# Output projection by seven products for each pair of channel tiles, h sums on VectorE, and early loads into pools that stay open

## The chip, the core and the metric

The kernel runs on one core of one Trainium2 chip, as one program. Its time is device microseconds. All figures in float32: weights and activations are float32 in HBM, and each number that TensorE multiplies is held as a pair of float32r tiles, a rounded high part and the rest.

TensorE (PE) multiplies, VectorE (DVE), ScalarE (ACT) and GpSimd (POOL) compute elementwise, SyncE (SP) issues the transfers in the order of its own queue. A static order of instructions stands for each engine; semaphores make an engine wait for another.

## The reference, cut to what matters

```python
z = h @ lp['w_in']                      # h: adaLN-modulated RMSNorm of x, (1024 tokens, 1024)
q = na_query(z, lp['q_norm_g'])         # 8 heads of 64
k, v = na_kv(z[..., A_K:A_Z], lp['k_norm_g'])
ya = neighbourhood_attention(q, k, v, kc, vc, lp['rpb']) * silu(z[..., A_Z:B_B])
yb = short_conv_branch(z, lp['conv_short_w'])
yc = conformer_branch(z, ...)           # 31-tap conv, layer norm, silu, gate
ga, gb, gc = jnp.split(jax.nn.sigmoid(z[..., GATES:]), N_BRANCH, axis=-1)
m = ga * (ya @ w_out_a) + gb * (yb @ w_out_b) + gc * (yc @ w_out_c)
x = x + gate * (m @ w_o)                # the output projection, 1024 x 1024 by 1024 x 1024
```

## The kernel before, in words

All activations lie transposed: 128 channels on the partitions, 1024 tokens along the free axis. h is kept in eight tiles ha (tokens 0 to 511) and eight tiles hb (512 to 1023), each with a high and a low half; hlf[o][k] is the tile of token half o and channel tile k. A product of two such pairs is three matmuls of 128x512 (high by high, high by low, low by high), in `mm3` or `product`.

The stages, by the span of the profiled execution: adaLN and the first projections to 123 us; four attentions, one for two heads each, with the projections for the next heads and the conv inputs as other work for TensorE, to 542; the Strassen stage to 943; the three merges to 1107; the output projection to 1195. A scheduler lays out each engine's order ahead of time from the program text, with its own timeline; `issue_after(x)` holds a group back until x is in the order. Tile pools decide which wait an instruction then needs: a tile with n buffers is given again only when the readers of the tile n before are done.

*Attention.* `attend(hp)` goes over 2 heads, 4 column blocks and 2 halves, so 16 half-steps for a pair of heads; they are counted 1 to 64 over the four attentions, and the last attention has 49 to 64. A half-step is sc and sl (scores of context and local window) on TensorE, mn and the local part of pbuf on VectorE (`TENSOR_REDUCE mn<-sc` opens it), two exponentials on ScalarE, pp (transposes by `ident`), ph and plo (the pair), py (the product with v), ya (its sum). GpSimd makes the bias image for it.

*Plain tiles.* `plain(ct, dst)` is a projection of h that ends in SiLU or Sigmoid: eight products into zaps for each token half (24 matmuls), `flt` from `tmp`, and a transfer out. ZA and BZ tiles stand in the text behind the last attention and two gate tiles stand later; the scheduler puts their matmuls between those of the last attention. zaps has two banks (ps_m); `tmp` is the pool rp with 6 buffers, shared by flt and hsum.

*h_sums(j)* makes the sums and differences of h blocks that the Strassen stage needs: four wholes (high + low), four differences, each stored to td. It is called once after each attention.

*Strassen stage.* A projection for two channel tiles and two token halves is a 2x2 block product; `group` and `last_two` do it by seven products (ga, gc, gd, ge and so on) instead of eight. T1 to T3 and T4 are the split td blocks: `load_t` brings each into a staging tile traw and splits it; T4 goes into the hb tiles 0 to 3. Weights come by wr, are split into wh and wl, and their block sums s stand on GpSimd. Beside it VectorE does the 31-tap conv (L690) and the results of the attention are gated (`a_result`, zb and a_result halves).

*Merges and projection.* `merge(1)`, `merge(0)`, `merge(2)` in this order: for each of eight channel tiles dm and token halves b, four products (ops) of wout with yb, ya or yc; mt sums them under the gates gs. The layer norm of the third branch (`norm_steps`, steps given out by `beside_b` and `beside_a`) runs beside the first two; its sums over channels are matmuls with ones (sums), its rstd is spread by matmuls with a diagonal (diag). yb and ya come back from DRAM through `loaded_y`, cv through cvin. Then for each of eight channel tiles and two token halves fin adds eight products of wo and the split mt (mh, ml), and L1116 does gate and residual.

Of the kernel before, what the change touches and what calls it, by code (L numbers as in the profile page):

```python
# [17 lines left out]
P = 128  # L18
D = 1024
KT = 8  # L20
# [22 lines left out]
def tile_hybrid(ctx: ExitStack, tc, x, xT, cx, cond, crow, ng, w_ada, b_ada, wqkv, wz,  # L43
# [5 lines left out]
    hctx = ExitStack()  # L49
    hp_pool = hctx.enter_context(tc.tile_pool(name="hT", bufs=1))  # L50
# [79 lines left out]
    def qkv(hp, w=None, cts=None, first=(), psc=None, mid=None):  # L130
# [41 lines left out]
        def context():  # L172
            vc = [a1.tile([P, 2, P], F32R, tag=f"vc{h}", name="vc") for h in range(2)]
# [64 lines left out]
    A_t = cst.tile([P, KT, 2], F32, name="A_t")  # L238
    B_t = cst.tile([P, KT, 2], F32, name="B_t")
# [224 lines left out]
    with tc.tile_pool(name="at", bufs=1, reuse_waits="tile") as at, \  # L464
# [45 lines left out]
        def attend(hp):  # L510
            ya = at.tile([P, 16, 64], F32, tag="ya", name="ya", bufs=1)
            for h in range(2):
# [9 lines left out]
                for cb in range(4):  # L522
# [54 lines left out]
                    dve.tensor_tensor(out=ya[hs, :, cb * 16 : cb * 16 + 16],  # L577
# [16 lines left out]
        def h_sums(j):  # L594

            def whole(o, k):
                t = tmp("hsum")
                pool.tensor_tensor(out=t, in0=hlf[o][k][:, 0].bitcast(F32), in1=hlf[o][k][:, 1].bitcast(F32), op=ALU.add)
                return t

            def less(i, a, b):

                pool.tensor_tensor(out=b, in0=a, in1=b, op=ALU.subtract)
                nc.sync.dma_start(td[i][j], b)
# [22 lines left out]

    sctx = ExitStack()
# [34 lines left out]
    for i in (1, 0, 2):  # L663
        load_t(T[i], i)
    load_t(T4, 3)
# [99 lines left out]

    def last_two(cts, uses):
# [24 lines left out]
        for n in two:  # L791
# [4 lines left out]
            dve.tensor_tensor(out=x[n], in0=f, in1=x[n], op=ALU.add)  # L796
        s3 = [s_(n, raw[n][0], raw[n][2], ALU.subtract, "s3") for n in two]
# [7 lines left out]
        for n in two:  # L805
# [5 lines left out]
            uses[n][1](0, y[n])  # L811
        s4 = [s_(n, raw[n][1], s2[n], ALU.subtract, "s4") for n in two]
# [90 lines left out]

    for i in range(4):
        u = b_start(i)
        gate_pair()
        b_end(i, u)
    halves = [(i, b) for i in range(4) for b in range(2)]
    for i in range(5):
# [5 lines left out]
        for _ in range(1 + (i in (0, 2, 4))):  # L915
            a_result(*halves.pop(0))
# [7 lines left out]
    hctx.close()  # L924


    wp = ctx.enter_context(tc.tile_pool(name="w2", bufs=9, side="right", reuse_waits="tile"))
    state["wp"] = wp
    kinds = (("mt", 8), ("cv", 4), ("ya0", 4), ("yb", 8), ("ya1", 4), ("bp", 0))
    pools = {n: (ctx.enter_context(tc.tile_pool(name=n, bufs=1, reuse_waits="tile")), k) for n, k in kinds}  # L930
    bp = pools["bp"][0]
# [3 lines left out]
    def big(name, n=S, dt=F32):  # L935
        return bp.tile([P, n], dt, tag="big", name=name, bufs=10)

    def of(kind, name, dt=F32R):
        p, k = pools[kind]
        return p.tile([P, S], dt, tag=kind, name=name, bufs=k)  # L940
# [13 lines left out]
    def loaded_y(n, i, name):  # L954
        out = []
        for h in range(2):
            t = of(("ya0", "ya1")[i // 2] if n else "yb", name)
            nc.sync.dma_start(t.bitcast(F32), ysd[n][i][h])
            out.append(t)
        return out  # L960

# [4 lines left out]
    def merge(br, ys, beside=lambda dm, b: None):  # L966
        for dm in range(KT):
            w = load_w(wout[br, dm], 4, dve if dm % 2 else pool)
# [233 lines left out]
```

## Time and profile before

| | us |
|---|---|
| median of 3 runs (lowest, highest) | 1202.31 (1201.91, 1203.02) |
| profiled execution, its span | 1200.33, 1198.5 |
| TensorE busy (share of the span) | 1126.9 (94%) |
| VectorE | 850.8 (71%) |
| ScalarE | 560.8 (47%) |
| GpSimd | 663.4 (55%) |
| HBM read, written | 120.62 MB, 46.14 MB |
| mean granted TensorE clock | 0.964 |

The prediction shows rows of several views. A stretch row gives start and end, its length, busy time and count of instructions for PE, PE weight loads, DVE, ACT and POOL, then the granted clock of TensorE, the mean busy share of the DMA engines and GB/s. A wait row gives the engine and line that waited, the one that ended the wait, and total us, times, longest. A row of a group gives the line, engine, operation and tiles, the count, and least, median and greatest duration in ns or, behind a bar, busy us and the mean. A row of the timeline begins with start and duration in us.

### The profile page before, as it was taken

How to read it: one execution, taken by the hardware profiler on the slowest of the kernel's cores; microseconds unless marked ns; L12 is line 12 of the kernel's file. 1: busy time of each engine (PE TensorE's matmuls, PEld its weight loads, DVE VectorE, ACT ScalarE, POOL GpSimd, SP SyncE). 2: the span in 40 equal slices, each digit the busy share in tenths (PEclk: the TensorE clock that was granted, in tenths of full speed). 3: DMA queues.
4: the chain of work that ended last, by engine and by line, in shares of the span. 5: the costliest groups of instructions: out<-in, count | busy, mean ns of one | idle time of the engine just before them, and what ended most of it. 6: DMA issues, size and time to landing. Idle time of an engine off the chain costs nothing.

```text
span 1198.5 us, 16663 instructions
## 1 busy us (share of the span) xinstructions
PE 1126.9 (94%) x5566; PEld 961.0 (80%) x5566; DVE 850.8 (71%) x1495; ACT 560.8 (47%) x1167; POOL 663.4 (55%) x623
## 2 busy tenths in 40 slices
PE   5779699999999999998999999999999798999998
PEld 4678699899899788886788888887877476888887
DVE  7995768788877875657993897896993356679311
ACT  5575358557656688784333332324334335313110
POOL 6675845645745833310887677868888006851110
PEclk7789899999999999999899999999999798999999
DMA  9235242332322313117234434345653694662621
GB/s 354 106 136 180 72 126 84 104 108 85 111 64 77 118 63 121 56 42 236 93 102 142 124 105 149 101 154 173 190 192 132 242 406 153 205 241 88 237 80 53
DMA packets 88151, 167.87 MB, mean 140 GB/s; under 512 B 11008, under 2 KB 39424, under 8 KB 88064
## 3 DMA queue, kind: packets, MB, share of 16 engines
q1 hardware_dynamic: 83456, 164.70, 40.9%
q10 hardware_dynamic: 4608, 2.10, 0.6%
q8 instruction: 44, 0.72, 0.3%
q14 instruction: 43, 0.35, 0.1%
HBM read 120.62 MB, written 46.14 MB: 139 GB/s over the span
## 4 chain that ended last, share of the span: by engine, by line
PE 59%; DVE 17%; DMA 8%; POOL 7%; issue 4%; ACT 3%; SPq 1%; POOLq 0%; DVEq 0%; ACTq 0%
DVE cv L690 4%; PE ops L107 4%; PE ops L109 4%; PE ops L108 4%; PE pp L564 3%; PE zaps L108 3%; PE zaps L107 3%; PE zaps L109 3%; PE ps L109 3%; PE ps L107 3%; PE ps L108 3%; PE fin L109 2%; PE fin L107 2%; PE fin L108 2%; DMA wada<-in_w_ada 2%
## 5 line engine op out<-in xcount | busy, mean ns | idle before, releaser
L90 POOL TENSOR_TENSOR wl<-wr,wh 128x384 fp32r<-128x384 f32 (+2 forms) x93 | 89.6, 969 | 182.2 <-ACT wh L88 156.1
L690 DVE SCALAR_TENSOR_TENSOR cv<-upad,cf_t,cv 128x512 f32<-128x512 f32 x240 | 166.9, 747 | 0.2
L88 ACT CAST wh<-wr 128x384 fp32r<-128x384 f32 (+2 forms) x138 | 61.2, 456 | 113.5 <-DMA wr<-in_wout 46.9
L533 POOL TENSOR_TENSOR bias<-mka,vimg 128x288 f32<-128x288 bf16 (+1 forms) x64 | 59.5, 931 | 87.8 <-DVE mn L547 76.5
L639 POOL TENSOR_TENSOR wl<-s,wh 128x512 fp32r<-128x512 f32 x57 | 79.5, 1409 | 11.1 <-ACT wh L638 6.4
L638 ACT CAST wh<-s 128x512 fp32r<-128x512 f32 x76 | 46.1, 616 | 75.6 <-POOL s L642 64.1
L639 POOL TENSOR_TENSOR wl<-wr,wh 128x512 fp32r<-128x512 f32 x46 | 64.4, 1402 | 22.7 <-ACT wh L638 22.7
L569 DVE TENSOR_TENSOR plo<-pp,ph 128x512 fp32r<-128x512 f32 (+1 forms) x96 | 60.8, 640 | 8.5 <-ACT ph L567 8.0
L714 PE MATMUL ga<-ha,wh 128*128 128x512 f32 x152 | 60.6, 398 | 6.5 <-ACT wh L638 4.7
L564 PE MATMUL pp<-ident,pbuf 128*128 128x128 f32 x352 | 59.1, 273 | 1.6 <-DVE pbuf L553 1.3
L716 PE MATMUL ga<-ha,wl 128*128 128x512 f32 x152 | 60.3, 397 | 0.2 <-POOL wl L639 0.2
L715 PE MATMUL ga<-ha,wh 128*128 128x512 f32 x152 | 60.2, 396 | 0.0
L567 ACT CAST ph<-pp 128x512 fp32r<-128x512 f32 (+1 forms) x96 | 51.7, 547 | 16.8 <-PE pp L564 16.0
L549 ACT ACTIVATE pbuf<-sc,mn 128x256 f32<-128x256 f32 x64 | 30.4, 475 | 60.1 <-DVE mn L547 59.6
L1116 DVE SCALAR_TENSOR_TENSOR o<-fin,gate,xr 128x512 f32<-128x512 f32 x16 | 12.0, 751 | 59.7 <-PE fin L109 59.7
L551 DVE TENSOR_TENSOR mn<-mn 128x1 f32<-128x1 f32 x64 | 17.6, 275 | 47.0 <-ACT pbuf L550 46.7
L109 PE MATMUL fin<-mh,wl 128*128 128x512 f32 x128 | 49.8, 389 | 0.0
L108 PE MATMUL fin<-ml,wh 128*128 128x512 f32 x128 | 49.8, 389 | 0.0
L107 PE MATMUL fin<-mh,wh 128*128 128x512 f32 x128 | 49.7, 389 | 0.0
L564 PEld LDWEIGHTS pp<-ident,pbuf 128*128 128x128 f32 x352 | 42.7, 140 | 7.0 <-DVE pbuf L553 2.6
L90 DVE TENSOR_TENSOR wl<-wr,wh 128x384 fp32r<-128x384 f32 (+2 forms) x45 | 31.6, 705 | 13.9 <-ACT wh L88 13.9
L79 POOL TENSOR_TENSOR ssh<-ssh,half_neg 128x4 f32<-128x4 f32 (+1 forms) x40 | 39.4, 987 | 2.7
(382 smaller groups left out, 3970.3 us busy)
## 6 DMA issues: line engine op xcount, KB each, us to landing
wr<-in_wz SPq DMA_DIRECT2D x36, 512.0 KB, 3.9
gs<-gd SPq DMA_DIRECT2D x24, 512.0 KB, 5.2
wada<-in_w_ada SPq DMA_DIRECT2D x16, 512.0 KB, 8.7
wr<-in_wz SPq DMA_DIRECT2D x36, 192.0 KB, 2.5
cht<-chd SPq DMA_DIRECT2D x24, 256.0 KB, 3.1
gd<-gate SPq DMA_DIRECT2D x22, 256.0 KB, 3.1
vimg<-in_rpbs SPq DMA_DIRECT2D x16, 288.0 KB, 3.0
gd<-c SPq DMA_DIRECT2D x18, 256.0 KB, 3.1
```

The lines of the kernel that those rows point to most:

```text
L88: act.copy(hi[:, :n], raw[:, :n])
L90: state["lo"] = lo_eng.tensor_tensor(out=lo[:, :n], in0=raw[:, :n], in1=hi[:, :n].bitcast(F32), op=ALU.subtract)
L107: pe.matmul(ps, ah, bh, start=i == 0, stop=False)
L108: pe.matmul(ps, ah, bl, start=False, stop=False)
L109: pe.matmul(ps, al, bh, start=False, stop=i == n - 1)
L564: pe.transpose(out=pp[:, c * 256 + hf * P : c * 256 + hf * P + P], in_=pts[hf][:, o : o + P], identity=ident)
L569: dve.tensor_tensor(out=plo[:, : m * 256], in0=pp[:, : m * 256], in1=ph[:, : m * 256].bitcast(F32), op=ALU.subtract)
L639: eng.tensor_tensor(out=lo, in0=src, in1=hi.bitcast(F32), op=ALU.subtract)
L690: dve.scalar_tensor_tensor(out=acc[b], in0=src, scalar=cf_t[:, i, j : j + 1], in1=acc[b], op0=ALU.mult, op1=ALU.add)
L714: pe.matmul(ps, wh, bh, start=first and j == 0, stop=False, skip_group_check=True)
L715: pe.matmul(ps, wh, bl, start=False, stop=False, skip_group_check=True)
L716: pe.matmul(ps, wl, bh, start=False, stop=last and j == 3, skip_group_check=True)
```

## The change

Four things change together.

- h_sums for all four j is called after the loop over heads, held back until the last ya of the third attention is in the order; its additions are VectorE's, not GpSimd's.
- The T blocks have a pool of their own (tp), opened before the Strassen stage and never closed, and load in place: the block comes into the low half and is split there. T1 to T3 load before the last two plain tiles, T4 at the first loop of the second half. The tiles of h (hT) stay open to the end.
- a_result is spread: one in each of three more loops instead of two in some. In last_two, yb is loaded after the f products and cvin before the last ones, into T and hb tiles; the first ya loads go with the merges' other tiles (`of`, `homes`). The layer-norm steps are cut and paced otherwise; the diagonal matmuls are one for each half.
- The output projection takes two channel tiles and both token halves as a 2x2 block product with seven products (fa, fc, fe, again fa, ff, fd, again fd): 84 matmuls instead of 96 for a pair. The block sums of wo are GpSimd's, those of m (MT1 to MT4) are made in merge(2) and by `third_sums`.

```diff
-                pool.tensor_tensor(out=t, in0=hlf[o][k][:, 0].bitcast(F32), in1=hlf[o][k][:, 1].bitcast(F32), op=ALU.add)
+                dve.tensor_tensor(out=t, in0=hlf[o][k][:, 0].bitcast(F32), in1=hlf[o][k][:, 1].bitcast(F32), op=ALU.add)
...
-                pool.tensor_tensor(out=b, in0=a, in1=b, op=ALU.subtract)
+                dve.tensor_tensor(out=b, in0=a, in1=b, op=ALU.subtract)
                 nc.sync.dma_start(td[i][j], b)
...
-            h_sums(hp)
             if hp < 3:
                 glu(hp + 1)
+                last = state["ya"].ins
+        with tc.issue_after(last):
+            for j in range(4):
+                h_sums(j)
...
-    T = [[pair(sp.tile([P, 2, 512], F32R, name=f"T{i}_{j}")) for j in range(4)] for i in (1, 2, 3)]
+    T = [[pair(tp.tile([P, 2, 512], F32R, tag=f"T{i}", name=f"T{i}", bufs=4)) for j in range(4)] for i in (1, 2, 3)]
...
-            t = s512("traw", "hs", 4)
-            nc.sync.dma_start(t, td[i][j])
-            split(*blocks[j], t, dve)
-
+            hi, lo = blocks[j]
+            nc.sync.dma_start(lo.bitcast(F32), td[i][j])
+            split(hi, lo, lo.bitcast(F32), dve)
+
+    for i in (1, 0, 2):
+        load_t(T[i], i)
     with tc.issue_after(state["py"].ins):
         for i in (6, 7):
             plain(GT + 2 * KT + i, gd[2 * KT + i], True)
-    for i in (1, 0, 2):
-        load_t(T[i], i)
-    load_t(T4, 3)
...
+    homes = {"mt": [f"ha{i}" for i in range(KT)], "cv": [f"hb{i}" for i in range(4)], "ya0": [f"hb{i}" for i in range(4, 8)],
+             "ya1": ["T3"], "yb": ["T1"] * 4 + ["T2"] * 4}
...
             dve.tensor_tensor(out=x[n], in0=f, in1=x[n], op=ALU.add)
+        yb_s.extend(loaded_y(0, i, "yb") for i in range(4))
...
+        for i in range(4):
+            t = of("cv", "cvin", F32)
+            nc.sync.dma_start(t, cvd[i])
+            cv.append(t)
         s4 = [s_(n, raw[n][1], s2[n], ALU.subtract, "s4") for n in two]
...
     for i in range(4):
         u = b_start(i)
+        if i == 0:
+            load_t(T4, 3)
         gate_pair()
+        if i:
+            a_result(*halves.pop(0))
         b_end(i, u)
...
-        for _ in range(1 + (i in (0, 2, 4))):
-            a_result(*halves.pop(0))
+        a_result(*halves.pop(0))
...
-    for dm in range(KT):
-        w = load_w(wo[dm], KT, pool if dm % 2 else dve)
...
-            mm3(ps, [(w[k][0], w[k][1], mfin[k][0][:, sl], mfin[k][1][:, sl]) for k in range(KT)])
...
+    def fin(d0):
...
+        a = fin_bank("fa")
+        product(a, w512(a11, pool), MB11, True, True)
+        p1 = part_sum("p1")
+        act.copy(p1, a)
+        pool.tensor_tensor(out=s1, in0=a21, in1=a22, op=ALU.add)
+        c = fin_bank("fc")
+        product(c, w512(s1, pool), MT1, True, True)
...
+        sub(pool, s2, s1, a11)
+        sub(pool, s4, a12, s2)
+        e = fin_bank("fe")
+        product(e, w512(s4, pool), MB22, True, True)
...
+        product(a, w512(a12, pool), MB21, False, True)
...
+        product(f, w512(s2, pool), MT2, True, True)
...
+        product(d, w512(s3, pool), MT3, True, True)
...
+        product(d, w512(wraw(wo[d0 + 1][:, B512[1]]), pool), MT4, False, True)
...
+    third_sums(MT2, "yb", b22, first)
+    f0, f1, f2, f3 = (fin(d) for d in (0, 2, 4, 6))
+    next(f0)
+    third_sums(MT3, "yb", b22, second)
+    next(f1)
+    third_sums(MT4, "mt", b21, first)
+    for f in (f0, f1, f0, f2, f1, f2, f3, f3, f2, f3):
+        next(f)
```

Three places in the order of the engines, each before and after the change (line, operation, written tile, read tiles, shape; the lines of after are its own). First VectorE in the last attention. Before, half-step 56 (`pbuf_` is a fixed tile of its probabilities):

```order
L544 TENSOR_REDUCE mn<-sc 128x1
L547 ISA pbuf_1395,mn<-sl,bias,mn 128x3x96
L547 ISA mn 128x1
L551 TENSOR_TENSOR mn<-mn 128x1
L552 RECIPROCAL mn<-mn 128x1
L553 TENSOR_SCALAR pbuf_1395<-pbuf_1395,mn 128x3x96
L554 TENSOR_SCALAR pbuf_1395<-pbuf_1395,mn 128x256
L591 TENSOR_TENSOR flt<-zaps,flt 128x512
```

After, from the first of the h sums on, where half-step 52 opens:

```order
L601 TENSOR_TENSOR hsum<-ha_175 128x512
L601 TENSOR_TENSOR hsum<-hb_463 128x512
L601 TENSOR_TENSOR hsum<-hb_682 128x512
L601 TENSOR_TENSOR hsum<-ha_179 128x512
L601 TENSOR_TENSOR hsum<-ha_176 128x512
L601 TENSOR_TENSOR hsum<-hb_517 128x512
L547 TENSOR_REDUCE mn<-sc 128x1
L554 TENSOR_TENSOR mn<-mn 128x1
L606 TENSOR_TENSOR hsum<-hsum 128x512
L572 TENSOR_TENSOR plo<-pp,ph 128x512 x2
L606 TENSOR_TENSOR hsum<-hsum 128x512
L550 ISA pbuf_1396,mn<-sl,bias,mn 128x4x96
```

The 32 h sums stand between half-steps 51 and 57, where one flt for each half-step stood; the first flt stands behind all but one of them.

TensorE at the same half-steps. Before, half-step 53:

```order
L564 MATMUL pp<-ident,pbuf_1391 128x128
L564 MATMUL pp<-ident,pbuf_1393 128x128
L541 MATMUL sl<-ks,qd 128x288
L539 MATMUL sc<-kc,qd 128x256
L540 MATMUL sc<-kc,qlz_1387 128x256
L542 MATMUL sl<-ks,qlz_1387 128x288
L107 MATMUL zaps<-hb_571,wh 128x512
L108 MATMUL zaps<-hb_571,wh 128x512
L109 MATMUL zaps<-hb_571,wl 128x512
```

After, half-step 56, behind which the fillers return:

```order
L567 MATMUL pp<-ident,pbuf_1392 128x128
L542 MATMUL sc<-kc,qd 128x256
L543 MATMUL sc<-kc,qlz_1388 128x256
L567 MATMUL pp<-ident,pbuf_1394 128x128
L106 MATMUL zaps<-hb_682,wh 128x512
L107 MATMUL zaps<-hb_682,wh 128x512
L108 MATMUL zaps<-hb_682,wl 128x512
```

After the change no zaps stands between the scores of half-step 49 and those of 56. From half-step 49 to 57 there are 142 instructions of TensorE, where there were 270.

Third, SP's queue at the entry of the merges (wr of in_wout are the merges' weights, gd the gates on their way out). Before:

```order
L86 DMA wr<-in_wout 128x384
L86 DMA wr<-in_wout 128x128
L951 DMA cvin<-cvd_129 128x1024
L951 DMA cvin<-cvd_130 128x1024
L837 DMA gd_153<-px 128x512
L951 DMA cvin<-cvd_131 128x1024
L951 DMA cvin<-cvd_132 128x1024
...
L958 DMA ya<-ysd_117 128x1024
...
L958 DMA yb<-ysd_109 128x1024
```

After:

```order
L789 DMA yb<-ysd_109 128x1024
...
L844 DMA cvin<-cvd_129 128x1024
...
L789 DMA ya<-ysd_117 128x1024
L789 DMA ya<-ysd_118 128x1024
L871 DMA gd_151<-px 128x512
L871 DMA gd_151<-gate 128x512
L789 DMA ya<-ysd_119 128x1024
L871 DMA gd_153<-gate 128x512
L967 DMA wr<-in_wout 128x512 x3
```

yb and cvin stand ahead of the last gates, and the weights of the merges behind three ya loads. The first of them wait for the products that read the tiles they write.

More of the change, by code (lines that the diff above doesn't have):

```diff
@@ L952, in loaded @@
         return t
[L954 to L960, printed above, removed]
     mt = [None] * KT
@@ L1026, in norm_steps @@
     def norm_steps():
-        cv.extend(loaded(cvd[i], "cvin", of("cv", "cvin", F32)) for i in range(4))
-        yield
         sums = []
@@ L1104, in tile_hybrid, with third_sums @@
         pass
-    for dm in range(KT):
-        w = load_w(wo[dm], KT, pool if dm % 2 else dve)
-        xr = big("xr")
-        nc.sync.dma_start(xr, xT[dm])
-        for b in range(2):
-            ps = ps_x.tile([P, 512], F32, tag="x", name="fin")
-            sl = B512[b]
-            mm3(ps, [(w[k][0], w[k][1], mfin[k][0][:, sl], mfin[k][1][:, sl]) for k in range(KT)])
-            o = tmp("o")
-            dve.scalar_tensor_tensor(out=o, in0=ps, scalar=gate[:, dm : dm + 1], in1=xr[:, sl], op0=ALU.mult, op1=ALU.add)
-            nc.sync.dma_start(out[dm, :, sl], o)
+    def third_sums(blocks, kind, a, b):
+        for j in range(4):
+            o = a(j) if kind == "mt" else b(j)
+            dve.tensor_tensor(out=o, in0=a(j), in1=b(j), op=ALU.subtract)
+            part(blocks, kind, j, o)
```

135 lines of the change are left out of this document (104 added, 31 removed).

## The prediction

> **What bounds the kernel now.** I read the page first, then the busy time by stretches, then who made TensorE wait. The page's engine line and clock row:
>
> ```profile
> PE 1126.9 (94%) x5566; PEld 961.0 (80%) x5566; DVE 850.8 (71%) x1495; ACT 560.8 (47%) x1167; POOL 663.4 (55%) x623
> PEclk7789899999999999999899999999999798999999
> ```
>
> TensorE is busy 94% of the span, so time can only come from fewer matmuls or from its idle stretches. A slice of the clock row is 30 us; counted from 0, its dips after the start are slice 4 (8), 19 (8), 31 (7) and 33 (8): behind idle time the granted clock falls, so they point to about 120, 570, 930 and 990 us. The stretches (us, then busy time and instructions of PE, PEld, DVE, ACT, POOL, granted clock, DMA share, GB/s) and the waits there:
>
> ```profile
> 123.10:140.80 17.70, 9.28 (x57) 8.98 (x55) 17.48 (x10) 8.27 (x21) 16.60 (x20) 0.86 0.27 80
> 140.80:149.20 8.40, 7.15 (x26) 6.82 (x26) 3.12 (x4) 0.42 (x1) 8.16 (x9) 0.68 0.17 55
> 437.00:486.70 49.70, 49.70 (x275) 43.13 (x275) 29.96 (x78) 41.86 (x81) 16.99 (x20) 1.00 0.26 87
> 540.60:545.40 4.80, 4.78 (x19) 3.97 (x20) 1.45 (x3) 0.41 (x2) 0.00 (x0) 0.66 0.47 163
> 570.29:576.13 5.84, 5.65 (x12) 4.01 (x13) 4.00 (x6) 2.55 (x5) 5.68 (x5) 0.50 0.55 215
> 942.90:962.00 19.10, 9.12 (x18) 4.33 (x18) 10.11 (x16) 9.27 (x18) 2.52 (x3) 0.64 0.99 365
> 962.00:1000.00 38.00, 33.73 (x134) 27.09 (x133) 20.18 (x51) 9.04 (x17) 3.28 (x4) 0.87 0.87 342
> ...
> PE sl L541 <- DVE ks L505: 8.4, 1, 8.4
> ...
> PE ga L714 <- ACT wh L638: 4.7, 1, 4.7
> PE py L573 <- DVE ya L577: 1.9, 1, 1.9
> ...
> PE sums L1006 <- ACT lnh L638: 7.7, 2, 7.2
> PE rstd L1052 <- DVE diag L1051: 4.2, 1, 4.2
> PE sums L1006 <- DVE cvin L1033: 2.3, 1, 2.3
> ```
>
> TensorE loses time at four places: the first boundary between heads (123 to 149), the end of attention (540), the entry of the Strassen stage (570) and the entry of the merges (943 to 1000). The attention stretch 437 to 486.7 loses nothing: there TensorE is full.
>
> One matmul, in the output projection:
>
> ```profile
> L107 PE MATMUL fin<-mh,wh x128: 388/389/390, 1107.6 to 1193.9; 128*128 128x512 f32 x128
> L109 PE MATMUL fin<-mh,wl x128: 388/389/390, 1108.0 to 1194.4; 128*128 128x512 f32 x128
> ```
>
> 389 ns is the time through the array; they overlap. From 1107.6 to 1194.4 there are 384 starts: 86.8 / 383 = 0.227 us a matmul. Where the granted clock is 0.50 (570.29:576.13) twelve take 5.84 us, 0.49 each.
>
> **The change, part by part.** The profiled execution took 1200.33 us; the median of the runs is 1202.31, 2.0 more. The sum is made against the former and given on top of the latter.
>
> *1. Sums off GpSimd at the first boundary.*
>
> ```profile
> 128.72 7.42 DVE L501 TENSOR_TENSOR qlz<-qT,qd 64x1024 fp32r<-64x1024 f32 x1
> 129.24 1.29 POOL L598 TENSOR_TENSOR hsum<-ha 128x512 f32<-128x512 f32 x1
> 130.49 2.50 POOL L598 TENSOR_TENSOR hsum<-hb 128x512 f32<-128x512 f32 x2
> ...
> L501 DVE TENSOR_TENSOR qlz<-qT,qd x8: 1218/1222/7415, 128.7 to 432.7; 64x1024 fp32r<-64x1024 f32 x8
> ...
> SPq L604 <- POOL hsum L603: 20.4, 3, 17.4
> ```
>
> This qlz takes 7.42 us where its median is 1.22, while GpSimd runs hsums and vc back to back; then TensorE waits 8.4 us for ks behind it, and SP's queue stands 17.4 us behind an hsum. The cause could also be the vc and bias instructions that stay on GpSimd. All of the excess of qlz is 6.2 us, half of it 3, and with the slow clock behind it (0.68 in 140.80:149.20, some 2.7 us of 8.4) up to 10. I take −6, range −3 to −10. The other three boundaries show no wait of TensorE: −0.5.
>
> *2. The same 32 instructions on VectorE, inside the last attention.* The order puts all of them between half-steps 51 and 57 (of 64; the last attention begins with 49). They take the same six "tmp" buffers as flt; so the first flt of the plain tiles comes only behind them, both banks of ps_m stay full, and TensorE has no filler. Between half-steps 49 and 57 it gets 142 instructions, where it had 270: 128 filler matmuls are moved behind. Those half-steps before:
>
> ```profile
> 437.01 0.42 DVE L544 TENSOR_REDUCE mn<-sc 128x1 f32<-128x256 f32 x1 [0.34 <-PE sc L540]
> ...
> 486.73 0.41 DVE L544 TENSOR_REDUCE mn<-sc 128x1 f32<-128x256 f32 x1
> ...
> L591 DVE TENSOR_TENSOR flt<-zaps,flt 128x512 f32<-128x512 f32 x7 | 4.8, 692 | 6.1 <-ACT flt L589 6.1
> ...
> L639 DVE TENSOR_TENSOR lnl<-sq,lnh x8: 680/686/694, 961.6 to 981.4; 128x512 fp32r<-128x512 f32 x8
> ...
> L642 DVE TENSOR_TENSOR s<-wr,s 128x512 f32<-128x512 f32 x8 | 11.6, 1449 | 8.1 <-POOL s L642 8.0
> ...
> L533 POOL TENSOR_TENSOR bias<-mka,vimg 128x384 f32<-128x384 bf16 (+1 forms) x8 | 6.7, 833 | 13.6 <-DVE mn L547 13.1 <-PE zaps L108 0.4
> ...
> DMA to landing us min/median/max: 2.0/2.4/4.2
> ```
>
> (The last row is for the 16 transfers from hsum.) 49.7 us for the eight half-steps, TensorE full; without the 128 matmuls its work is 49.7 − 128 × 0.227 = 20.6 us. VectorE has 29.96 us there; less five of the seven flt (3.4), plus 32 hsums at 0.686 (the nearest row with two inputs in SBUF) = 22.0: 48.5 us. So the stretch keeps its length, about 48.5 us, and TensorE idles 28, plus 1 to 2 for a lower clock behind the gaps: **+29**. Bounds: if the hsums overlapped at 0.6 and filled waits, 44 us, +24; if GpSimd's bias instructions (6.7 us there) and the transfers out of hsum tiles (2.4 us to landing; one tile is written again only after its transfer) stand in between, 56, +36. The 128 matmuls are not lost; they follow later at full rate, so that idle time counts whole. SP issues 16 transfers of td there; what stands behind them (weights of plain tiles, bias images) waits for VectorE in order, and nothing needs it before the plains go on. ACT is relieved: without the alternation of Sigmoid and Exp the order has 30 table loads for 46. That gives nothing while VectorE sets the pace.
>
> The row says something more. L642 on VectorE with two SBUF inputs takes 1449 ns, where GpSimd works in the same pair. The Trainium skill, "SBUF — State Buffer", section "Who interferes with whom", says that a VectorE instruction with two SBUF inputs and a GpSimd instruction that reads SBUF shut each other out for the whole instruction, whoever is first. It thereby credits term 1 and charges term 2: by it each bias instruction can hold one hsum, and the sum would end near the upper bound, +36. The qlz row agrees with it.
>
> *3. End of attention.* The moved fillers stand behind it, so the wait for ya (1.9) and the slow clock of 540.60:545.40 (about 1.4) are covered: −3.3 (0 to −3.3).
>
> *4. Entry of the Strassen stage.* The T blocks load into their own tiles before the last two plain tiles; the staging buffers go. The first wz weights still stand on SP behind the four loads of the T4 blocks, which wait for the plains' last reads of hb, so part of the 4.7 us stays. With the slow clock (5.84 against 12 × 0.227 = 2.7) 7.8 us are there; I take −2.5 (0 to −6).
>
> *5. Strassen stage.* The attention results are spread one to a loop over more loops.
>
> ```profile
> PE gd L714 <- DVE c L720: 2.7, 2, 1.6
> PE ga L714 <- ACT p L738: 1.0, 1, 1.0
> ```
>
> TensorE waits about 5 us between 825 and 943; −1 (+1 to −3).
>
> *6. From the last Strassen product to the end.*
>
> ```profile
> 942.57 0.39 PE L716 MATMUL ge<-hb,wl 128*128 128x512 f32 x1
> ...
> 962.04 2.77 PE L107 MATMUL ops<-yb,wh 128*128 128x512 f32 x6
> ...
> L958 SPq DMA_DIRECT2D yb<-ysd x8: 319/320/430, 952.6 to 959.0; - x8
> ...
> 925.00:942.00 17.00, 17.00 (x77) 14.09 (x76) 5.75 (x9) 4.05 (x7) 0.00 (x0) 1.00 0.25 94
> ...
> L86 SPq DMA_DIRECT2D wr<-in_wout x12: 332/333/688, 942.7 to 993.0; - x12
> ...
> DMA to landing us min/median/max: 2.2/7.5/9.4
> ...
> 1194.82 0.75 DVE L1116 SCALAR_TENSOR_TENSOR o<-fin,gate,xr 128x512 f32<-128x512 f32 x1 [4.69 <-PE fin L109]
> ```
>
> From 942.96 (end of the last ge) to 1194.8 are 251.8 us. In it are 992 wide matmuls (32 sums, 576 ops, 384 fin), 225.2 us; 26.6 are lost. The reason is in the yb row: these loads are issued at 952.6 to 959.0, in a stretch that moves 365 GB/s at a DMA share of 0.99.
> After the change yb, two of the ya tiles and cvin load during last_two, into T and hb tiles; the norm's first sums are no longer first on TensorE. What stays: the wout weights still stand on SP behind loads that wait for the last product; load (2.2 us at the least), split and first matmul come to 4 to 6, and some 3 of slow clock: 8. The GpSimd work that is pressed into the second merge, 2 (0 to 7). fin: seven products of 12 matmuls for each of four pairs, 336 for 384: −48 × 0.227 = −10.9. Its GpSimd work for a pair is 12 instructions; at 1.27 us (its 128x512 sums) 15.3, at the costlier split of the row below 16.9, against 84 × 0.227 = 19.1 us of TensorE: it stays covered, with 2 (0 to 5) for single stalls.
>
> ```profile
> L639 POOL TENSOR_TENSOR wl<-s,wh 128x512 fp32r<-128x512 f32 x57 | 79.5, 1409 | 11.1 <-ACT wh L638 6.4
> ```
>
> VectorE splits for the third sums, 24 instructions of 0.69, beside the first pairs' 19 us. The tail is one addition longer, +0.7. The sum: 944 × 0.227 = 214.3, + 8 + 2 + 2 + 0.7 + 1.5 for rstd = 228.5, against 251.8: **−23** (−16 to −27).
>
> Sum: −6 − 0.5 + 29 − 3.3 − 2.5 − 1 − 23 = **−7.3**: 1193.0 for an execution like the profiled one, 1195.0 on the median.
>
> **Rivals.**
> *A, slower: VectorE becomes the bound for longer.* If an hsum among bias instructions and its own transfers costs more than 0.92 us, the stretch passes 56 us and the gain is gone. For it: L642's 1449 ns; at the mean of the two rows, 1.07, term 2 is 29 + 32 × 0.38 = 41 and the time 1207; at 1449 throughout it is 53 and 1219. Against: of GpSimd's 16.99 us there only 6.7 are bias; its weight splits move behind with the plain tiles. The Trainium skill's rule gives the lower part of this case, 1195 + 7 = 1202.
> *B, much faster: the hsums lie in VectorE's waits.* VectorE idles 19.7 of those 49.7 us. If TensorE gets its fillers back after two half-steps in fact and not after six, the loss is some 12 and the time 1178. Against it: the order is static, and the first flt stands behind 31 of the 32 hsums.
> *C, the early loads don't come early.* yb needs the f products' last reads, ya's need e's, and wout stands behind the latter. If the 19.1 us gap stays, 11 of term 6 are gone: 1206. For: 0.99 DMA share there now. Against: just before it, 925.00:942.00, the DMA share is 0.25.
> *D, no change to be told:* errors of terms 2 and 6 cancel, 1200 to 1204.7.
>
> **How the numbers follow.** Forecast (1183 to 1200) 0.54, A above 1204.7 0.19, C 0.06, B 0.08, D 0.13. A measurement tells 0.2%, 2.4 us, from no change. Faster: 0.54 + 0.08 = 0.62; same 0.13; slower 0.25. The likeliest time is 1195; its own range is 1185 to 1203 by the terms' bounds; for 8 in 10 it reaches into A and C on one side and towards B on the other: 1181 to 1209.
>
> **What would show it.** Term 1: qlz at 1.2 us, TensorE's wait for ks below 3 us. Term 2: between the eight half-steps VectorE near full, TensorE below half, waits for sc, sl or pp on VectorE of 20 us or more; if TensorE is above 80% there, term 2 is wrong and the time is near B. Terms 3 and 4: no wait for ya; a wait for the first wh of 1 to 4 us. Term 6: yb issued before the last product, a gap of 4 to 8 us at the first ops; fin in 336 matmuls with TensorE above 95%. The forecast fails upward if hsums take over 0.9 us, or if GpSimd holds fin.

## The result and the profile after

The changed kernel takes 1231.21 us (median of 4 runs, 1227.24 to 1234.08), the kernel before 1202.11 (4 runs, 1199.33 to 1203.02): ratio 1.0244, 95% interval 1.0208 to 1.028. It is slower by 29 us; 7 us less were forecast, and the range ended at 1209. The profiled execution took 1232.85 us; its span is 1231.1, which is 32.6 us more than that of before (1198.5), and the table below adds up to these 32.6.

The page of after, its engine line and clock row:

```profile
PE 1131.3 (92%) x5506; PEld 960.7 (78%) x5506; DVE 895.8 (73%) x1539; ACT 554.6 (45%) x1151; POOL 712.2 (58%) x627
PEclk7789999999999868999899999999899899999799
```

There are 60 matmuls fewer, and yet TensorE is busy 4 us longer: its matmuls take longer where the clock is low, and the clock is low where it waits. GpSimd, relieved of 32 sums, is busy 49 us longer. The clock row has dips that before had not: slices 13 to 15 (400 to 492 us), 28 (862 to 893) and 37 (1139 to 1170).

The span of each, cut at first and last starts of TensorE's matmuls (rows like those of fin in the prediction); us from cut to cut:

| from, to | before | after | difference | forecast |
|---|---|---|---|---|
| start, first zaps (plain tiles) | 413.5 | 402.4 | −11.1 | −6.5 |
| first zaps, last zaps | 151.7 | 184.9 | +33.2 | +25.7 |
| last zaps, first ga | 5.1 | 4.4 | −0.7 | −2.5 |
| first ga, last ge (Strassen stage) | 372.3 | 380.4 | +8.1 | −1 |
| last ge, first ops | 19.4 | 6.9 | −12.5 | |
| ops: three merges | 58.4 + 43.6 + 43.4 | 53.4 + 45.3 + 51.7 | +5.0 | |
| last ops, last fin (seven products) | 87.0 | 96.6 | +9.6 | |
| last fin, end | 4.1 | 5.1 | +1.0 | last four: −23 |

The last four rows sum to +3.1. Waits of TensorE in after (those of the opening stage left out), and stretches as in the prediction:

```profile
PE sl L544 <- DVE mn L550: 8.8, 6, 3.2
PE py L577 <- DVE plo L572: 7.9, 3, 5.0
...
PE ops L106 <- ACT wh L645: 6.5, 1, 6.5
...
PE ga L721 <- ACT p L745: 5.7, 1, 5.7
...
PE fe L721 <- ACT mb L645: 3.9, 1, 3.9
PE fe L722 <- DVE mb L646: 3.7, 2, 2.6
...
423.50:477.10 53.60, 35.92 (x143) 28.79 (x143) 45.37 (x110) 21.10 (x56) 13.76 (x11) 0.62 0.30 110
477.10:523.00 45.90, 45.87 (x248) 39.30 (x247) 27.02 (x71) 37.45 (x71) 12.82 (x14) 1.00 0.22 69
...
972.50:979.00 6.50, 0.04 (x1) 0.00 (x0) 0.69 (x1) 1.25 (x2) 0.00 (x0) 0.88 0.95 290
...
1077.60:1129.50 51.90, 46.61 (x194) 36.52 (x192) 51.80 (x51) 10.30 (x17) 43.16 (x26) 0.97 0.60 211
1129.50:1150.00 20.50, 10.22 (x36) 6.44 (x34) 20.40 (x20) 8.05 (x15) 16.16 (x11) 0.87 0.21 68
```

423.50 to 477.10 are half-steps 49 to 57: 143 matmuls where 275 stood, at a granted clock of 0.62. The third merge and the first 20 us of the projection have a full VectorE (51.80 of 51.90, 20.40 of 20.50). The third merge before, for comparison:

```profile
1064.00:1107.50 43.50, 43.50 (x193) 35.88 (x192) 39.78 (x58) 14.12 (x30) 15.49 (x15) 1.00 0.39 128
```

### The profile page after: what moved, and what is told of

Its sections match the earlier page's. It is cut to its first block, busy times and chain, and to the rows that moved or that the text cites. A ratio compares the mean times of both kernels' runs of the same rounds, so it can differ in the third digit from the quotient of the medians.

```text
span 1231.1 us, 16561 instructions
## 1 busy us (share of the span) xinstructions
PE 1131.3 (92%) x5506; PEld 960.7 (78%) x5506; DVE 895.8 (73%) x1539; ACT 554.6 (45%) x1151; POOL 712.2 (58%) x627
## 5 line engine op out<-in xcount | busy, mean ns | idle before, releaser
L646 POOL TENSOR_TENSOR wl<-wr,wh 128x512 fp32r<-128x512 f32 x70 | 101.4, 1451 | 111.2 <-ACT wh L645 110.9
L646 POOL TENSOR_TENSOR wl<-s,wh 128x512 fp32r<-128x512 f32 x73 | 106.1, 1466 | 7.9 <-ACT wh L645 7.1
L645 ACT CAST wh<-s 128x512 fp32r<-128x512 f32 x92 | 55.8, 616 | 116.5 <-POOL s L649 98.2
L89 POOL TENSOR_TENSOR wl<-wr,wh 128x384 fp32r<-128x384 f32 (+1 forms) x57 | 57.7, 1019 | 78.7 <-ACT wh L87 67.0
L645 ACT CAST wh<-wr 128x512 fp32r<-128x512 f32 x90 | 55.4, 618 | 52.0 <-PE ops L107 19.2
L1017 POOL TENSOR_TENSOR mt<-mt,gs 128x512 f32<-128x512 f32 x24 | 37.1, 1550 | 16.3 <-DVE gs L1016 16.3
L721 PEld LDWEIGHTS ga<-ha,wh 128*128 128x128 f32 x152 | 29.6, 195 | 17.0 <-ACT p L745 6.5
L87 ACT CAST wh<-wr 128x384 fp32r<-128x384 f32 (+1 forms) x66 | 31.1, 486 | 26.0 <-PE psc L189 7.6
L746 POOL TENSOR_TENSOR s<-wr 128x512 f32<-128x512 f32 x17 | 23.1, 1359 | 32.1 <-DMA wr<-in_wz 32.1
L547 DVE TENSOR_REDUCE mn<-sc 128x1 f32<-128x256 f32 x64 | 26.6, 416 | 18.7 <-PE sc L543 18.2
```

The lines of the kernel that those rows point to most:

```text
L89: state["lo"] = lo_eng.tensor_tensor(out=lo[:, :n], in0=raw[:, :n], in1=hi[:, :n].bitcast(F32), op=ALU.subtract)
L645: act.copy(hi, src)
L646: eng.tensor_tensor(out=lo, in0=src, in1=hi.bitcast(F32), op=ALU.subtract)
L721: pe.matmul(ps, wh, bh, start=first and j == 0, stop=False, skip_group_check=True)
L1017: (pool if br == 0 or b == 0 else dve).tensor_tensor(out=mt[dm][:, sl], in0=mt[dm][:, sl], in1=gs[:, sl], op=ALU.add)
```

## The experiments

All ratios are to runs of the kernel before on the same chip; times are medians. All edits are to the changed kernel or to the one named.

### Where the 33 us of the last attention are

**hs_back: the sums on GpSimd, after each attention.**

```diff
-                dve.tensor_tensor(out=t, in0=hlf[o][k]...
+                pool.tensor_tensor(out=t, in0=hlf[o][k]...
-        with tc.issue_after(last):
-            for j in range(4):
-                h_sums(j)
+            h_sums(hp)
```

> The changed kernel, but the h sums go back to GpSimd and to their places after each attention. Theory (the sums on VectorE inside the last attention starve TensorE of filler): the stretch from half-step 49 to 57 goes back from 53.5 to about 50 us with its 128 filler matmuls inside, so 33 us come back, and the first boundary costs its 10 us again: about 1208. Rival (the last attention is slow for another reason, such as the T loads or the pools that stay open): it stays at 1225 to 1231, and the boundary makes it 1235 or more.

1211.12 us, 1.0068 (1.0041 to 1.0094); about 1208 was forecast. First to last zaps take 150.1 us again (before 151.7), every half-step begins within 0.9 us of its time in the kernel before, and TensorE waits 8.4 us for ks at the first boundary again. So the sums alone make both the gain of 11 and the loss of 33; neither T tiles nor pools do.

**hs_pool_late: the sums at the new place, on GpSimd.**

> The changed kernel with the sums at their new place in the last attention, but on GpSimd. If VectorE's load is what holds TensorE there, the loss of 33 us is mostly gone: 1200 to 1208. If it is the six buffers that the sums share with flt (32 x 1.29 us on GpSimd, 41 us, in which no flt gets a buffer), TensorE still lacks its fillers between half-steps 49 and 57: 1225 to 1240.

1225.95 us, 1.0191 (1.0156 to 1.0226). First to last zaps: 176.4 us. Of the 33 us, 25 stay when the sums are off VectorE. That speaks for the buffers; the engine is worth some 8.

**hs_own: the sums on VectorE, late, in buffers of their own.**

```diff
-    rp = ctx.enter_context(tc.tile_pool(name="rp", bufs=6, side="right"))
+    rp = ctx.enter_context(tc.tile_pool(name="rp", bufs=3, side="right"))
...
-                t = tmp("hsum")
+                tag, n = ("hs1", 1) if (o, k) == (0, j) else ("hs2", 2)
+                t = rp.tile([P, 512], F32, tag=tag, name="hsum", bufs=n)
```

> The changed kernel, sums on VectorE at their new place, but in three buffers of their own; flt keeps three. The order then has 176 plain matmuls between half-steps 49 and 57, where the changed kernel has 20. If the shared buffers starved TensorE, most of the 33 us come back and the boundary's gain of 10 stays: 1198 to 1204. If VectorE's load of sums holds the attention, at most the 8 us between the two late versions on VectorE and GpSimd are to be had: 1222 to 1231.

1214.44 us, 1.0091 (1.0055 to 1.0128): between the two forecasts. The stage it was made for went as the buffers' theory said: first to last zaps 156.6 us, 28 of the 33 back, TensorE full beside VectorE's sums:

```profile
423.00:470.00 47.00, 47.00 (x249) 40.33 (x248) 40.30 (x84) 36.52 (x70) 19.55 (x21) 1.00 0.39 131
```

What is missing to the forecast is at the start: the first zaps come at 409.3 (after 402.4). There three buffers stand for six in the opening stages too, and VectorE reaches the first heads' qlz at 135.9 us instead of 128.9. That the three buffers do this was not run apart.

**hs_inter: the same six buffers, another order in the text.**

```diff
-        with tc.issue_after(last):
-            for j in range(4):
-                h_sums(j)
-        for i in range(4):
-            plain(ZA + i, zad[i])
-        for i in range(4):
-            plain(BZ + i, zbd[i])
+        for i in range(8):
+            plain(ZA + i if i < 4 else BZ + i - 4, (zad + zbd)[i])
+            if 0 <= i < 4:
+                h_sums(i - 0)
```

> The changed kernel with one edit: the text calls h_sums(j) behind the plain tile ZA+j, not all four ahead of the plain tiles. Engine, place in time, and the six shared buffers stay. Theory (buffers of a pool go round in the order of the text: flt, which stands behind 16 sums in the text, gets none until the sums are done): now flt and sums alternate, TensorE keeps its fillers (161 plain matmuls between half-steps 49 and 56, where the changed kernel has none), the 28 to 33 us come back and the 7 us of the first boundary stay gained: 1198 to 1204. Rival (six buffers are too few for both, or VectorE is full): 1215 or more.

1209.57 us, 1.006 (1.0043 to 1.0078). The edit also drops the hold of the sums, which is more than the expectation says; they still run between half-steps 48 and 56, and hs_own, which keeps the hold, got 28 us back in this stage. First to last zaps: 158.7 us, and the first zaps stay early, 404.0. 26 of the 33 us come back with the same engine, buffers and place. Its first stretch:

```profile
404.00:480.00 76.00, 73.13 (x390) 61.40 (x389) 65.28 (x137) 54.88 (x109) 27.66 (x28) 1.00 0.38 131
```

VectorE is busy 65.28 of 76 us and TensorE loses 3. The total is 6 us above the forecast's upper end, since the other stages did not gain: the Strassen stage took 382.8 and the projection 97.8. What the two edits show is that this pool gives its buffers in the order of the text. Of the 32 sums 16 take a new buffer from it (the differences are written in place). In the changed kernel flt stands behind these 16 and gets no buffer before they have theirs. TensorE has run 48 zaps matmuls by half-step 49, which fills both banks, and only 21 more follow up to half-step 57, the first of them at 468.0.

### Strassen stage, third merge, projection

**ares_back: a_result at its old places.**

```diff
         gate_pair()
-        if i:
-            a_result(*halves.pop(0))
         b_end(i, u)
...
-        a_result(*halves.pop(0))
+        for _ in range(1 + (i in (0, 2, 4))):
+            a_result(*halves.pop(0))
```

> The changed kernel with the gating of the attention results (a_result) back at its old places in the Strassen stage. Theory: the wait of TensorE of 5.7 us for p, with 3 us of slow clock behind it, comes from a yain load on SP ahead of a weight load; both go and the Strassen stage is 372 to 375 us instead of 381: about 1224. Rival (the stage lost time to GpSimd's work elsewhere): no change, 1229 to 1233.

1224.95 us, 1.0186 (1.0163 to 1.021). The Strassen stage takes 371.2 us (380.4) and the wait for p is 0.5 us, within 1 us of the forecast; 2 us are lost again at the entry of the merges (8.8 us for 6.9). The cause, in the timeline of after (start, duration; in brackets the idle time and who ended it) and in SP's waits there:

```profile
867.43 0.86 SPq L702 DMA_DIRECT2D cvd<-cvo  x2
872.29 0.32 SPq L898 DMA_DIRECT2D yain<-yad  x1
872.70 1.15 SPq L738 DMA_DIRECT2D wr<-in_wz  x1
...
SPq L898 <- DMA cvd<-cvo: 3.9, 1, 3.9
...
878.67 1.26 POOL L746 TENSOR_TENSOR s<-wr 128x512 f32<-128x512 f32 x1 [7.94 <-DMA wr<-in_wz]
...
881.19 0.62 ACT L645 CAST ysh<-yain 128x512 fp32r<-128x512 f32 x1 [8.96 <-POOL yain L900]
882.24 0.57 ACT L745 COPY p<-ga 128x512 f32<-128x512 f32 x1
...
882.87 0.80 PE L721 MATMUL ga<-ha,wh 128*128 128x512 f32 x1 [5.75 <-ACT p L745]
```

yain and cvo share the four `ev` buffers. The moved yain load waits on SP until a cvo tile has been sent, 3.9 us; behind it stands a weight load, for which GpSimd waits 7.94 us; yain's product stands behind that on GpSimd, ysh behind it on ScalarE, and behind ysh the copy p that frees TensorE's bank. A wait of 3.9 us on a queue became 5.75 on TensorE and a lower clock after it.

**gate_early: the gate's sums in the second merge.**

```diff
     def beside_a(dm, b):
         for _ in range(1 + b):
-            if next(steps, 0) == 0:
-                next(gsteps, None)
+            next(steps, None)
+        next(gsteps, None)
```

> The changed kernel with one step of the gate's column sums (gw, a VectorE instruction of 2.2 us each) given out at each half of the second merge, as it was before, instead of behind the last step of the layer norm. Theory (eight gw of 17 us and their collisions with GpSimd overfill VectorE in the third merge, and the third sums queue behind): the third merge goes from 51.7 to 45 to 47 us and the start of the projection loses 5 us less: 1216 to 1222. Rival (the splits and third sums alone overfill VectorE): within 3 us of 1231.

1224.83 us, 1.0175 (1.0139 to 1.0211): between the two forecasts. The third merge takes 47.6 us (51.7), the projection from the last ops 93.6 (96.6); the forecast of 5 us there was too much. So 4.1 of the 8.3 us that the third merge lost come back. Of the rest, 2.4 us are one wait of TensorE for ych, which the layer norm makes. The rows of gw, the gate's column sums, of before, after and this run (least, median, greatest in ns, first and last start):

```profile
L1082 DVE CUSTOM_DVE_ANT_0 gw<-gw,crs x8: 1214/1242/2044, 1044.1 to 1067.4; 128x1024 f32<-128x1024 f32 x8
...
L1134 DVE CUSTOM_DVE_ANT_0 gw<-gw,crs x8: 1215/2304/2333, 1077.4 to 1100.1; 128x1024 f32<-128x1024 f32 x8
...
L1134 DVE CUSTOM_DVE_ANT_0 gw<-gw,crs x8: 1214/1437/2312, 1022.4 to 1059.7; 128x1024 f32<-128x1024 f32 x8
```

In after all eight lie in the third merge (1077.4 on), and take 2304 ns in the median: GpSimd is busy 43 of 52 us there. Those are two ways in which the merge is overfull, later work and slower work.

**fin8: the output projection of before.**

```diff
-    third_sums(MT2, "yb", b22, first)
-    f0, f1, f2, f3 = (fin(d) for d in (0, 2, 4, 6))
...
+    for dm in range(KT):
+        w = load4(wo[dm][:, B512[0]], ...) + load4(wo[dm][:, B512[1]], ...)
...
+            mm3(ps, [... for k in range(KT)])
```

> The changed kernel with the output projection of before (eight products, 384 matmuls, sixteen splits of mt), its tiles in the new homes and its weights in the new pool. Theory (VectorE cannot make the twelve third sums and their splits beside the end of the merges): TensorE's idle time at the start of the projection goes, fin takes 87 us instead of 95 and the third merge 44 to 46 instead of 52: 1215 to 1222. Rival (GpSimd's weight sums hold the projection, or nothing but the count of matmuls matters): 1242, 48 more matmuls.

1224.29 us, 1.0188 (1.0155 to 1.0221). Eight products are 7 us faster than seven here, and the projection takes 90.7 us from its first matmul on (94.5); 87 and a total of 1215 to 1222 were forecast. The third merge stayed at 51.7: it isn't what seven products add that fills it, against my theory (gate_early shows half of what does).

### The mends together

**all_own, all_each_head, mend3.** hs_own, the sums on VectorE after each attention, and hs_inter, each with the edits of ares_back and gate_early.

> Three mends together: the sums in buffers of their own, a_result at its old places, the gate's steps in the second merge. If the three losses are separate and add: 1231 - 30 - 6 - 11 = 1184, below the kernel before. If they hide one another (time regained in one place lost in the next), 1195 to 1205.

> The same three mends, but the sums on VectorE, in the shared buffers, at their old places after each attention instead of in buffers of their own. There they meet flt of the conv inputs and the next heads' work. If the engine is what mattered at the first boundary (GpSimd's sums beside qlz), the gain of 10 us there stays: 1184 to 1190. If VectorE is too busy at the boundaries: 1195 to 1205.

> The interleaved sums, with a_result at its old places and the gate's steps in the second merge. If the losses add: 1231 - 30 - 6 - 6 = 1189; against the kernel with buffers of its own and the same two mends (1198) it has the boundary's 7 us more. If the boundary's gain is lost later, 1195 to 1200.

all_own: 1198.17 us, 0.9958 (0.994 to 0.9976), the rival's case. all_each_head: 1207.95, 1.0042 (1.0022 to 1.0062), outside what either theory gave: its first to last zaps take 165.5 us, and at the first boundary (141 to 149) the clock is 0.50. mend3: 1194.57, 0.9944 (0.9927 to 0.996), just below the rival's 1195 to 1200. Against the sum forecast for it, 1189, 6 us are missing: 4 in the last attention (159.2 us, where 30 less than 184.9 were forecast) and 2 in the entry of the merges (8.9 us instead of 6.9).

**mend4: fewer additions on GpSimd in the second merge.**

```diff
-                    (pool if br == 0 or b == 0 else dve).tensor_tensor(out=mt[dm]...
+                    (pool if b == 0 else dve).tensor_tensor(out=mt[dm]...
```

> The same and one more edit: in the second merge the additions of the second token half go to VectorE, GpSimd has only those of the first. Theory (GpSimd is full in the second merge, 39 of 45 us, so the layer norm's products come late and VectorE idles for them and has too much afterwards): 16 fewer GpSimd instructions of 1.3 us, the third merge falls from 47.6 to 44 to 45.5 us and the projection's start loses less: 3 to 6 us below mend3. Rival (both engines read SBUF and shut each other out, so it doesn't matter on which the addition stands): within 2 us.

1191.66 us, 0.9915 (0.99 to 0.993), 2.9 below mend3, their runs not overlapping; but the third merge is 47.1 against 47.5, so not by the way forecast. The projection is 1.4 us shorter. The spans of the two profiled executions are only 0.6 us apart, so the rest isn't seen in a stage. The edit moves 8 additions, not the 16 of the expectation: GpSimd has 16 of them instead of 24.

**mend3_fin8: mend3 with eight products.**

> As mend3, with the output projection of before (eight products, 384 matmuls). If the seven products give what is left of 10.9 us after idle time at the start (fin 92.8 against 90.7 us in earlier runs of both), the two are even within 3 us: the seven products as built are worth nothing. If the seven products were worth their 48 matmuls: mend3 + 8 to 11.

1186.62 us, 0.9874 (0.9858 to 0.989): 8 us below mend3, where one forecast had the two even and the other had this kernel 8 to 11 us above. fin takes 86.8 us with TensorE full, against 92.8 for 48 matmuls fewer.

### Why seven products are not faster

In mend3 VectorE's timeline at the start of the projection shows differences for the third sums (L1159) ahead of the products of the merge's last tile (L1011) and of the MB splits (L642; MB11 to MB22 are the blocks of m as they stand, MT1 to MT4 their sums):

```profile
1101.45 0.68 DVE L1011 TENSOR_TENSOR gs<-ops,gs 128x512 f32<-128x512 f32 x1
1102.16 1.03 DVE L1012 TENSOR_TENSOR mt<-mt,gs 128x512 f32<-128x512 f32 x1
1103.12 1.76 DVE L642 TENSOR_TENSOR mb<-mt,mb 128x512 fp32r<-128x512 f32 x1
1104.80 3.42 DVE L1159 TENSOR_TENSOR mt<-mt 128x512 f32<-128x512 f32 x2
1108.14 0.68 DVE L1011 TENSOR_TENSOR gs<-ops,gs 128x512 f32<-128x512 f32 x1
...
1109.47 0.80 PE L718 MATMUL fe<-mb,wh 128*128 128x512 f32 x1 [5.07 <-DVE mb L642]
```

**thirds_late, thirds_late_bal, thirds_out.** On mend3: the third sums held until the last MB split is in the order; the same on mend4; and mend3 without third sums, whose products are then made with the MB blocks in their place, so that it is a bound and does not compute the projection.

```diff
-        eng.tensor_tensor(out=lo, in0=src, in1=hi.bitcast(F32), op=ALU.subtract)
+        state["split"] = eng.tensor_tensor(out=lo, in0=src, in1=hi.bitcast(F32), op=ALU.subtract)
...
-    third_sums(MT2, "yb", b22, first)
...
+    with tc.issue_after(state["split"].ins):
+        third_sums(MT2, "yb", b22, first)
+        third_sums(MT3, "yb", b22, second)
+        third_sums(MT4, "mt", b21, first)
```

> mend3 with one edit: the third sums (MT2 to MT4, 12 differences and 12 splits) are held back until the last split of MB22 is in the order. In mend3 nine of the differences, 13.3 us of VectorE with GpSimd beside them, stand ahead of the last gs products and of the MB22 splits, for which fe and fa wait (5.1, 2.9, 2.8 us). Theory (the order of VectorE's work is what idles TensorE at the start of the projection): these waits fall below 4 us together, fin goes from 92.8 to 80 to 85 us, and the time to 1182 to 1187. Rival (the amount of VectorE's work is too much wherever it stands): the waits move to ff and fd behind the first pairs' other products, fin stays at 90 or more, 1192 to 1196.

> The same on mend4 (in the second merge VectorE adds the second token half). Theory: 2 to 3 us below thirds_late, as mend4 was below mend3: 1179 to 1185. Rival: no difference to thirds_late.

> mend3 without the third sums: MT2 and MT3 are replaced by the blocks MB22, MT4 by MB21, so 24 VectorE and 12 ScalarE instructions are left out, and the projection's products are made with other operands. This is a bound for what the third sums cost. Theory: the waits at the start of fin are all due to them: fin 78 to 81 us, 1180 to 1183. Rival (GpSimd's weight sums or the splits of MB hold the start): fin 88 or more, 1190 or more.

1191.33 us (0.9887, 0.9846 to 0.9927), 1186.97 (0.9863, 0.9826 to 0.99), 1185.69 (0.9841, 0.9804 to 0.9879). The second is 4.4 us below the first, where 2 to 3 were forecast, with one of its runs inside the other's range; the third lies between its two forecasts. fin: 91.7, 88.6, 85.2 us, mend3 92.8. The order alone is worth 1 us in fin (the medians of thirds_late and mend3, on two chips, are 3 us apart): the waits for fe fall from 8.0 to 5.9 us, and a wait of fd for VectorE's v of 3.7 us comes in their place. That is the rival's case. Without third sums at all, fin still takes 8.9 us more than its 336 x 0.227 = 76.3; so the third sums are 7.6 of the 16.5 us lost in mend3. The rest lies at the handover from the third merge:

```profile
PE fe L717 <- ACT mb L641: 3.9, 2, 3.2
PE fe L718 <- DVE mb L642: 2.0, 2, 1.5
```

These are all of TensorE's waits in the projection of thirds_out, 5.9 us; the other 3 are, by my estimate, the lower clock behind them. Seven products need MB21 and MB22 of all four last channel tiles within their first 48 matmuls; the end of the third merge yields them too late. thirds_late_bal is even with mend3_fin8 (1186.97 and 1186.62 us, ratios 0.9863 and 0.9874): the best version with seven products here is no faster than the one with eight, which doesn't have mend4's edit. Eight products with that edit were not run.

## Why the prediction was wrong, step by step

The forecast was −7.3 us for the profiled execution, and 32.6 more were measured, so the forecast was 39.9 us off. By steps: −4.6 at the first boundary, 7.5 in the last attention, 1.8 at the entry of the Strassen stage, 9.1 in that stage and 26.1 from its end on.

*1, first boundary: right in sign, small in size.* qlz is down from 7.42 to 1.22 us, TensorE's wait for ks from 8.4 to 1.3. The gain is 11.1 for 6.5, beyond the bound of 10 by 0.6 with the other boundaries: 7.0 us at the first half-step, and 2.7 more by half-step 17. The rule that the prediction cited, the Trainium skill's "SBUF — State Buffer", "Who interferes with whom", agrees with hs_back, where the sums on GpSimd bring the 8.4 us back. But leaving GpSimd is not enough: in all_each_head, with the sums on VectorE and still behind each attention, qlz takes 1.23 us, and yet the first half-step begins only 2.2 us earlier than before; with the sums late and on GpSimd (hs_pool_late) it begins 8.5 us earlier. What gained was that the sums left the boundary.

*2 and 3, last attention: right in sign and mechanism, 7.5 us low.* The stretch took 53.6 us, inside the bounds (44 to 56), for 48.5. Not through dear sums: an hsum took what I had assumed,

```profile
L601 DVE TENSOR_TENSOR hsum<-ha x8: 665/682/693, 434.2 to 462.1; 128x512 f32<-128x512 f32 x8
L606 DVE TENSOR_TENSOR hsum<-hsum x16: 670/675/1223, 438.3 to 470.7; 128x512 f32<-128x512 f32 x16
```

with one of 16 near twice its time. The collisions came all the same, and GpSimd paid for them: one bias image of 0.92 us in the median took 4.19 while five sums ran, of which three stand here,

```profile
447.90 4.19 POOL L536 TENSOR_TENSOR bias<-mka,vimg 128x288 f32<-128x288 bf16 x1 [5.29 <-DVE mn L550]
448.34 0.68 DVE L606 TENSOR_TENSOR hsum<-hsum 128x512 f32<-128x512 f32 x1
448.94 0.68 DVE L601 TENSOR_TENSOR hsum<-ha 128x512 f32<-128x512 f32 x1
449.54 0.68 DVE L601 TENSOR_TENSOR hsum<-hb 128x512 f32<-128x512 f32 x1
```

and no engine waited for that image. VectorE had 45.37 us of work and 8.2 idle: 5.7 of them waiting for sc, 2.1 for a transfer out of an hsum tile. With the clock at 0.62 TensorE's 143 matmuls took 35.92 us instead of 20.6, and VectorE waited for it too. I had counted the low clock only behind the stretch, not inside it. Counted by plain matmuls (133 of them moved out of the stretch, 24 out of the 21 us ahead of it) the stretch lost 53.6 - (49.7 - 133 x 0.227) = 34.1 us for 29, the fillers' end ahead of it 3.0 that I had not counted, and the covered end of the attention gave 3.9 back for 3.3 (no wait for ya).

I also named VectorE as the bound of that stretch, with the buffers as the reason that fillers lack. hs_own and hs_inter show that the buffers decide most of it, 26 to 28 of the 33 us: with flt among the sums, VectorE carries them at a cost of about 7.

*4, entry of the Strassen stage:* −0.7 for −2.5. The wait for the first wh is 4.0 (4.7 before), in the forecast range: T4 loads on SP still stand ahead of it.

*5, Strassen stage: wrong in sign.* I gave the spread of a_result −1 us (+1 to −3) out of the 5 us that TensorE waited there, and 8.1 were lost. The step that failed is the one not taken: the loads that move with a_result were not followed on SP, and one of them held a weight load.

*6, the end: wrong by 26 us, the largest term.* Its first part was right: the entry of the merges fell from 19.4 to 6.9 us (forecast gap 4 to 6 and 3 of slow clock). Of the 26 us, 18.5 lie behind the last ops (96.6 us for 87.0 − 10.9 + 2) and 8 in the second and third merge (10 lost for 2). What failed:
- "2 (0 to 7)" for GpSimd in the second merge. The merges lost 5.0 net, the third alone 8.3. The layer norm's steps were given out later, and the gate's only behind them; gw fell into the third merge, which VectorE had filled to 91% before.
- "24 instructions of 0.69, beside the first pairs' 19 us": this is the step that weighs most. The sum put these 16.6 us of VectorE at nothing, taking it to be free there. It was still behind with the third merge and full (20.40 of 20.50 us), so the products waited for the MB blocks, and beside GpSimd's weight sums its instructions took longer: in mend3 nine differences took 13.3 us. Left out, the third sums give 7.6 of the 16.5 us back that mend3 loses in fin (thirds_out); the rest is MB blocks that come late, and the low clock behind the waits. GpSimd, which I had named as the danger, held TensorE up in fin once: 1.7 us before the first fa, where wh waited for a weight sum.
- 10.9 us for 48 matmuls. It is what TensorE saves when it is full; of the 94.5 us of fin it was idle or slow for 18.

*Rivals.* A said: the stretch passes 56 us. It didn't, and the time is still above A's 1207, so none of the rivals had the cause: C's gap closed. I asked whether VectorE would be the bound in the one stretch that I knew to be dear, and not in the stage of the largest gain. A named the right engine, for another stretch.

## What to carry to other kernels

A pool hands out its buffers in the order of the text: a burst of long-lived tiles ahead of a producer's output tile takes the output away from TensorE's filler, though the burst's own engine has room; put their uses in the text in turn. When a change saves matmuls by adding elementwise sums, the stage before it decides: if VectorE is behind with its work when that stage ends, the first products wait for it and the saving is spent at a lower clock. For each moved step follow its loads on the queue of transfers, and what stands behind them.

## What the runs showed of the hardware that was not expected

- VectorE's gw (two inputs from SBUF, 128x1024) takes 1.24 us in the median where GpSimd is busy 13.66 of 24 us (before) and 2.30 where it is busy 19.79 of 24.6 (after); the MB splits of after take from 0.67 to 1.78 us, 1.16 in the median. Beside the h sums it was GpSimd that lost: 4.19 us for a bias image of 0.92. The Trainium skill's "SBUF — State Buffer", "Who interferes with whom", says that two such instructions shut each other out and that the order of issue decides which one waits; both cases agree with it.
- In 423.50:477.10 TensorE is busy two thirds of the time and waits four times for 2.6 to 5.0 us. The granted clock is 0.62 there, and 143 matmuls took 15 us more than the 20.6 estimated for a full clock. The Trainium skill's "TensorE: Matmul & The Clock Gate", section "HAM oscillation — how this bites in real kernels", tells of waits over some 3.4 us between matmuls, each of which lowers the clock. Here one wait was that long (5.0 us, to 439.7); the clock then stood at 0.50 from 442 to 472, through waits of 3.2 us at the most.
